# Value rows shifted by one token inside SBUF on ScalarE's queue, and the next dense job's first weights loaded a piece sooner

## The chip, the cores and the metric

The kernel runs on one core of a Trainium2 chip. The core has TensorE (PE, matmuls), VectorE (DVE), ScalarE (ACT), GpSimd (POOL) and SyncE (SP), which here only issues transfers. Sixteen DMA engines move data between DRAM and SBUF, the on-chip memory of 128 partitions. The metric is the device time of one execution in microseconds (us); lower is better.

## The reference

One layer of an encoder over 2048 tokens of width 1024: adaptive RMS norm, one input projection to two groups of eight heads, stick-breaking attention for the first group and chunked softmax attention for the second, an output projection, and a squared-ReLU MLP. The change touches the values of the first group:

```python
h = rmsnorm(x, g_norm1[l]) * (1.0 + sc1) + sh1
proj = h @ w_in[l]
q_sb, k_sb, v_sb, q_ca, k_ca, v_ca = jnp.split(proj, split_pts, axis=-1)
...
    suffix = lax.cumsum(log_1m_beta, axis=3, reverse=True) - log_1m_beta
    w = jnp.where(strict, jnp.exp(log_beta + suffix), 0.0)
    outs.append(jnp.einsum('bhqk,bkhd->bqhd', w.astype(v.dtype), vb))
```

## The kernel before

Tokens are stored in reverse order, in four blocks (`tb` 0 to 3) of `TB` = 512 tokens, each of four tiles of 128 tokens. fp32 products are made of three matmuls on a high and a low part, which the kernel produces with a cast on ACT and a subtraction on DVE (`split`).

A stick-breaking weight is a difference of two neighbouring running products. The kernel doesn't form these differences of weights; it multiplies the running products with differences of values, v(next row) - v(row), and adds the first row of each tile at the end (`vcol`). So for every value tile (`vr`, 128 tokens by 512 columns) it needs the same tile moved up by one row (`vn`). Row 127 of `vn` is the first row of the next tile, and for a block's last tile the first row of the block that was computed before. In the old kernel the whole tile is written to DRAM (`scr_r`) and read back one row further (`raw_rows`, `next_rows`).

The work runs in stages:

- **Projection stage** (about 0 to 443 us). A list of jobs (feature group, piece, block) is run by `run_job`. Piece 4 holds the first group's values; its jobs (0, 4, 3), (0, 4, 2) and, as the last job of all, (1, 4, 1) go through `step_values`. PE fills one of four PSUM banks for each tile; ACT copies it to `vr`; SP issues the write and the read; POOL subtracts; ACT and DVE split the result into `sv`; SP stores it. Two small queues of work, `behind` and `later`, run a piece of work a given number of tiles after it was added. With (0, 10, 2) the norm of block 0 begins: its x goes into the buffers that block 1's x leaves, ACT squares it, DVE sums (`nsaa`), and PE needs the sums (`pva`).
- **Attention stage** (about 443 to 1700 us). Units of scores, sigmoid, scan, transposes and value products, with the rest of the projections and the output projections as filler matmuls between them (`Filler`, `fill_qkv`, `outproj`). The values of block 0 are made here by `late_values`, in two halves of 256 columns, two tiles at a time (`vrf`, `vnf`).
- **MLP stage**, which the change doesn't touch.

PE, ACT, DVE and POOL keep the written order through the class `Ordered`, whose line L42 stands for most instructions in the profile. SP keeps the written order up to the attention stage; after that a scheduler arranges SP's issues. The framework gives the transfers of SP's and ACT's queues, in the order of the program, eight semaphores in turn. A transfer therefore waits on its queue until the transfer eight places before it, on whichever queue, is complete. All loads and stores of the names above are SP's; ACT's queue carried nine transfers.

A filler's weights go through a ring of three buffers (tag `r8`); a piece needs two of them. Inside a job the next piece's two loads are issued during the last tile of a piece (L1020). The first two of a new job are issued when the job starts, after its activations `fx` (L1005 here, in `fill_qkv`):

```python
            ht = self.moving()
            ...
            nxt = [load(pieces[0], i) for i in range(2)]
            yield "wait" if tb == 0 else "start"
```

Of the kernel before, what the change touches and what calls it, by code (L numbers as in the profile page):

```python
# [18 lines left out]
P = 128  # L19
# [60 lines left out]
def encoder_kernel(ctx, tc, xT, c, g1, g2, w_in, w_rest, gqk, bias, w_o, w1, w2, w_ada, b_ada, out):  # L80
# [31 lines left out]
    scr_r = dram.tile([S + P, NH * HD], F32, name="scr_r")  # L112
    scr_h = dram.tile([P, KT, 2, TB], F32, name="scr_h")

    ident = cpool.tile([P, P], F32, name="ident")
# [102 lines left out]
        )  # L218


    def raw_rows(tb, t, n, cols):

        r = tb * TB + t * P
        return scr_r[r : r + n * P, cols].rearrange("(t p) e -> p t e", p=P)

    def next_rows(tb, t, n, cols):

        r = tb * TB + t * P + 1
        return scr_r[r : r + n * P, cols].rearrange("(t p) e -> p t e", p=P)

    def first_values(tb, pairs):

        for pr in pairs:
            src = scr_r[tb * TB : (tb + 1) * TB, pr * P : (pr + 1) * P].rearrange("(i r) p -> p i r", r=P)[:, :, 0:1]
            sp.dma_start(vcol[:, pr, 4 * tb : 4 * tb + 4].unsqueeze(2), src)

    stores, drain = [], []
# [16 lines left out]
    if True:  # L254
# [178 lines left out]
                        later.add(3 + n // 2, lambda n=n: turn(n))  # L433
                yield

        waiting, halves = [], []

        def step_values(tb, tt, ps, nm):

            raw = stp.tile([P, TB], F32, tag="qh", name=f"vr{nm}_{tt}", bufs=6)  # L440
            act.copy(raw, ps)
            sp.dma_start(raw_rows(tb, tt, 1, slice(None))[:, 0], raw)
            waiting.append((tt, raw))
            for n in range(1 if tt < 3 else 2):
                if waiting[0][0] == tt and tt < 3:
                    break
                t, r = waiting.pop(0)
                behind.add(2 + n, lambda t=t, r=r: follow(tb, t, r, nm))
            if tt == 3:
                behind.add(2, lambda: first_values(tb, range(NH // 2)))  # L450

        def follow(tb, t, raw, nm):

            nx = stp.tile([P, TB], F32, tag="qh", name=f"vn{nm}_{t}", bufs=6)
            sp.dma_start(nx, next_rows(tb, t, 1, slice(None))[:, 0])

            def less():
                pool.tensor_tensor(nx, nx, raw, op=ALU.subtract)

            def parts():  # L460
                if t % 2 == 0:
                    halves[:] = [
                        stp.tile([P, NH // 2, 2, 2, HD], F32R, tag="st", name=f"sv{nm}_{t}_{hf}") for hf in range(2)
                    ]
                for hf, sv in enumerate(halves):
                    half = nx[:, hf * CW : (hf + 1) * CW].rearrange("p (h d) -> p h d", d=HD)
                    split(sv[:, :, t % 2, 0, :], sv[:, :, t % 2, 1, :], half)
                    if t % 2:
                        sp.dma_start(
                            scr_v[0, tb, hf][:, :, t - 1 : t + 1, :].rearrange("h p t e -> p h (t e)"),  # L470
                            sv.rearrange("p h t l d -> p h (t l d)").bitcast(F32),
                        )

            behind.add(1, less)
            behind.add(2, parts)

        def prepare_wo(n):
            raw = stp.tile([P, KT, P], F32, tag="bg", name=f"wo{n}", bufs=2)
# [164 lines left out]
        osp.dma_start(scr_r[S, :].rearrange("(p f) -> p f", p=P), vcol[:, 0, : NH * HD // P])  # L643

        todo = [(1.5, lambda j=j: ada(j)) for j in range(2 * KT, 6 * KT)]
        for i in range(NH):
# [66 lines left out]
    if True:  # L713
# [253 lines left out]
        class Filler:  # L967


            def __init__(self, make, *x):  # L970
                self.tiles = []
                self.gen = make(self, *x)
                self.src = next(self.gen)

            def fetch(self, n):

# [16 lines left out]

        def fill_qkv(self, tb, ht, pieces):

            self.tiles = ht or []
            yield None if ht else lambda k: scr_h[:, k]
            ht = self.moving()

            def load(piece, i):  # L1000
                w = ring.tile([P, KT // 2, 2, CW], F32R, tag="r8", name=f"fw{tb}_{piece}_{i}")
                sp.dma_start(w.bitcast(F32), scr_w[piece,][:, i * 4 : i * 4 + 4, :, :])
                return w

            nxt = [load(pieces[0], i) for i in range(2)]  # L1005
            yield "wait" if tb == 0 else "start"
            for n, piece in enumerate(pieces):
                grp, hf = divmod(piece, 2)
                w, nxt = nxt, []
                for j in range(2):  # L1010
                    if n == len(pieces) - 1 and j:
                        yield "ahead"
                    nm = f"f{tb}_{piece}_{j}"
                    ps = dense.tile([P, TB], F32, tag="ps", name=f"p{nm}")
                    last = 0 if grp < 2 else 1
                    for tt in range(last + 1):
                        tl = slice((2 * j + tt) * P, (2 * j + tt + 1) * P)
# [24 lines left out]
                    yield keep  # L1042
# [3 lines left out]
        def late_values(tb, hf, j, ps, nm):  # L1046

            cols = slice(hf * CW, (hf + 1) * CW)
            raw = raws[j] = fp.tile([P, 2, CW], F32, tag="vr", name=f"vr{nm}", bufs=2)
            act.copy(raw, ps.rearrange("p (t c) -> p t c", t=2))  # L1050
            sp.dma_start(raw_rows(tb, 2 * j, 2, cols), raw)
            if not j:
                return
            for i in range(2):
                later.add(1 + i, lambda i=i, raw=raws[i]: late_follow(tb, hf, i, raw, nm))
            later.add(2, lambda: first_values(tb, (2 * hf, 2 * hf + 1)))

        def late_follow(tb, hf, j, raw, nm):

            nx = xrp.tile([P, 2, CW], F32, tag="xr", name=f"vn{nm}_{j}")  # L1060
            sp.dma_start(nx, next_rows(tb, 2 * j, 2, slice(hf * CW, (hf + 1) * CW)))

            def less():
                pool.tensor_tensor(nx, nx, raw, op=ALU.subtract)
# [5 lines left out]
            later.add(1, less)  # L1070
            later.add(2, parts)

        stepped = set()

        def outproj(self, g):
            yield lambda k: scr_m[g, k]

            def load(n):
                w = ring.tile([P, 2, KT, P], F32R, tag="r8", name=f"ow{g}_{n}")
                sp.dma_start(w.bitcast(F32), scr_wo[n,])  # L1080
                return w

            mx = self.moving()
            ws = [load(0), load(1)]
            rx = load_residual(g, 0, xrp)
            yield "wait"
            for n in range(KT):
# [2 lines left out]
                    resident[n] = w  # L1090
                if n + 2 < KT:
                    ws.append(load(n + 2))
                if n + 1 < KT:
                    rx = load_residual(g, n + 1, xrp)
                else:
                    yield "ahead"
# [59 lines left out]
        def fill(part):  # L1156
# [5 lines left out]
            while credit >= 1 and filler and not rest:  # L1162
# [3 lines left out]
                elif got == "ahead":  # L1166
                    for f in filler[1:2]:
                        f.ahead()
                elif callable(got):
# [611 lines left out]
```

## Time and profile before

| | us |
|---|---|
| median of 3 runs (2689.1 to 2690.29) | 2689.9 |
| the profiled execution | 2689.82 |
| its span, first to last instruction | 2688.0 |

| engine | busy us | share |
|---|---|---|
| PE | 2583.0 | 96% |
| DVE | 1884.6 | 70% |
| ACT | 1417.6 | 53% |
| POOL | 604.2 | 22% |

In the page's forty slices of 67.2 us the DMA engines' busy share is highest in the projection stage:

```profile
DMA  9779977988887678775778777796675343465574
```

Each digit is tenths of the 16 DMA engines' time. A row of a group or of the timeline names engine, operation, and the tiles written and read (`out<-in`); behind a bracket or a bar stands the idle time ahead of it and what ended it.

### The profile page before, as it was taken

Reading aid. Unit: us, or ns where it says so; the run is one execution under the profiler, and the core shown is the slowest. Engines: PE = TensorE matmul, PEld = TensorE weight load, DVE = VectorE, ACT = ScalarE, POOL = GpSimd, SP = SyncE. Lnnn points to the kernel's source line nnn. Section 1 sums busy time; section 2 is a strip of 40 time slices with the busy share of each in tenths; the row PEclk is TensorE's granted clock in tenths of the full one; section 3 lists DMA queues with packets and bytes.
Section 4 is the critical chain, followed back from the end, with each engine's and each line's share of the span. In section 5 each row is a group of like instructions: output and inputs, shape, how many; then the busy total and the mean of one; then the engine's idle time right before and its main releaser. Section 6 shows DMA issues by size and latency. Waiting matters only on the chain. (4 is left out here: it accounts for less than half of the span.)

```text
span 2688.0 us, 38753 instructions
## 1 busy us (share of the span) xinstructions
PE 2583.0 (96%) x12816; PEld 2163.1 (80%) x12816; DVE 1884.6 (70%) x3222; ACT 1417.6 (53%) x2722; POOL 604.2 (22%) x617
## 2 busy tenths in 40 slices
PE   6999797899899899999999999999999999999999
PEld 5888686779788788878888888878888888888887
DVE  6655574678689787989758878767857565655565
ACT  5333333776676577656665444456544444444443
POOL 4331142421430134111442232200001323200000
PEclk9999898999999899999999999999999999999999
DMA  9779977988887678775778777796675343465574
GB/s 344 299 299 346 343 282 250 285 259 256 265 258 252 210 228 288 226 246 184 218 258 295 271 265 260 254 335 216 219 270 188 138 164 138 149 243 191 201 266 157
DMA packets 277272, 659.59 MB, mean 245 GB/s; under 512 B 38736, under 2 KB 72528, under 8 KB 267216
## 3 DMA queue, kind: packets, MB, share of 16 engines
q1 hardware_dynamic: 275776, 652.40, 71.3%
q10 hardware_dynamic: 1296, 4.72, 0.4%
q8 instruction: 101, 1.65, 0.3%
q14 instruction: 99, 0.81, 0.1%
HBM read 461.44 MB, written 195.56 MB: 244 GB/s over the span
## 5 line engine op out<-in xcount | busy, mean ns | idle before, releaser
L42 PE MATMUL ps<-oph,opv 128*128 128x512 f32 x2688 | 612.3, 389 | 0.2
L42 PE MATMUL ps<-h,opw 128*128 128x512 f32 x2664 | 606.3, 390 | 2.6 <-DVE cx L42 2.6
L42 PEld LDWEIGHTS ps<-oph,opv 128*128 128x128 f32 x2688 | 503.8, 188 | 106.8 <-DVE opv L42 1.2
L42 PEld LDWEIGHTS ps<-h,opw 128*128 128x128 f32 x2664 | 501.0, 188 | 107.6 <-DVE cx L42 3.5
L42 ACT CAST wth<-wt 128x512 fp32r<-128x512 f32 (+3 forms) x544 | 257.1, 483 | 215.3 <-PE wt L42 205.7
L42 DVE TENSOR_TENSOR wtl<-wt,wth 128x512 fp32r<-128x512 f32 (+3 forms) x544 | 291.3, 547 | 82.0 <-ACT wth L42 79.9
L42 DVE TENSOR_TENSOR oph<-hw,oph 128x512 fp32r<-128x512 f32 x224 | 156.2, 697 | 221.0 <-ACT oph L42 221.0
L42 PE MATMUL pt<-w,ht 128*128 128x512 f32 x1248 | 291.5, 393 | 2.8 <-DVE qh L42 2.2
L42 ACT CAST oph<-hw 128x512 fp32r<-128x512 f32 x224 | 139.3, 622 | 282.8 <-PE ps L42 264.8
L42 PEld LDWEIGHTS pt<-w,ht 128*128 128x128 f32 x1248 | 234.5, 189 | 52.5 <-ACT csq L42 2.9
L42 DVE TENSOR_TENSOR_SCAN p<-z,p,zero 128x512 f32<-128x512 f32 x192 | 245.4, 1278 | 34.9 <-ACT z L42 33.9
L42 PE MATMUL acc<-wth,v 128*128 128x512 f32 (+3 forms) x544 | 222.0, 412 | 2.3 <-DMA v<-scr_v 2.3
L42 PE MATMUL z<-k,q 128*128 128x512 f32 (+3 forms) x640 | 186.8, 374 | 29.9 <-DVE p L42 27.5
L42 ACT ACTIVATE z<-z 128x512 f32<-128x512 f32 (+1 forms) x320 | 166.2, 520 | 60.2 <-PE z L42 54.9
L42 POOL TENSOR_TENSOR ts<-w 128x512 f32<-128x512 f32 x32 | 46.0, 1437 | 662.3 <-DMA w<-in_w_dram 557.0
L42 PE MATMUL acc<-wtl,v 128*128 128x512 f32 (+3 forms) x544 | 186.3, 349 | 0.0
L42 DVE TENSOR_TENSOR opw<-w,opw 128x512 fp32r<-128x512 f32 x127 | 101.8, 803 | 113.0 <-ACT opw L42 112.8
L42 POOL TENSOR_TENSOR e<-e,cols 128x640 f32<-128x640 f32 (+4 forms) x128 | 143.0, 1123 | 163.4 <-DVE cols L42 84.0
L42 PE MATMUL wt<-ident,p 128*128 128x128 f32 x1088 | 172.2, 274 | 4.4 <-DVE cols L42 2.9
L42 PEld LDWEIGHTS wt<-ident,p 128*128 128x128 f32 x1088 | 134.8, 141 | 35.3 <-DVE cols L42 5.7
L42 PE MATMUL po<-fx,ow 128*128 128x512 f32 x576 | 160.3, 393 | 0.0
L42 PEld LDWEIGHTS z<-k,q 128*128 128x128 f32 x640 | 115.1, 191 | 52.5 <-DVE p L42 31.5
(197 smaller groups left out, 3963.9 us busy)
## 6 DMA issues: line engine op xcount, KB each, us to landing
hw<-scr_hid SPq DMA_DIRECT2D x112, 512.0 KB, 4.1
k<-scr_k SPq DMA_DIRECT2D x272, 128.0 KB, 4.3
v<-scr_v SPq DMA_DIRECT2D x136, 256.0 KB, 3.8
q<-scr_q SPq DMA_DIRECT2D x128, 256.0 KB, 5.1
w<-in_w_dram SPq DMA_DIRECT2D x64, 512.0 KB, 5.4
hw<-scr_s SPq DMA_DIRECT2D x64, 512.0 KB, 4.6
fw<-scr_w SPq DMA_DIRECT2D x28, 1024.0 KB, 6.9
wa<-in_w_ada_dram SPq DMA_DIRECT2D x48, 512.0 KB, 6.2
```

Of the source, the lines that this page charges most:

```text
L42: return lambda *x, **y: self.tc.keep_in_program_order(f(*x, **y))
```

## The change

1. In `step_values` and `late_values` the tile `vn` is made without DRAM. ACT's queue issues one transfer of 127 rows from `vr` to `vn`, one row higher (`step_down`), and one for the last row, from the next tile's first row (`step_over`). The first row of each tile goes to a small DRAM tensor `scr_f` (`first_row`), from which a block's last tile gets its last row (`next_block`) and `vcol` its columns. `scr_r`, `raw_rows` and `next_rows` are gone.
2. The subtraction and the split stand at other places of `behind` and `later`, and `vcol` is read later.
3. A filler holds its first two weight loads in `firsts`. The filler that runs yields `"weight"` twice while its last piece runs, and the next one issues one load each time.

```diff
-    def raw_rows(tb, t, n, cols):
...
-    def next_rows(tb, t, n, cols):
...
+    def step_down(nx, raw):
+
+        act.dma_start(nx[0 : P - 1], raw[1:P])
+
+    def step_over(nx, raw):
+
+        act.dma_start(nx[P - 1 : P], raw[0:1])
...
         def step_values(tb, tt, ps, nm):
 
             raw = stp.tile([P, TB], F32, tag="qh", name=f"vr{nm}_{tt}", bufs=6)
+            if tb > 1:
+                nx = stp.tile([P, TB], F32, tag="qh", name=f"vn{nm}_{tt}", bufs=6)
+            elif tt % 2:
+                nx = before["pair"][:, 1]
+            else:
+                before["pair"] = stp.tile([P, 2, TB], F32, tag="bg", name=f"vn{nm}_{tt}", bufs=2)
+                nx = before["pair"][:, 0]
             act.copy(raw, ps)
-            sp.dma_start(raw_rows(tb, tt, 1, slice(None))[:, 0], raw)
-            waiting.append((tt, raw))
...
+            step_down(nx, raw)
+            act.dma_start(first_row(tb, tt, slice(None)), raw[0:1])
+            if tt:
+                step_over(before[tt - 1][1], raw)
+            before[tt] = raw, nx
+            if tt:
+                behind.add(1, lambda: follow(tt - 1, nm))
             if tt == 3:
-                behind.add(2, lambda: first_values(tb, range(NH // 2)))
-
-        def follow(tb, t, raw, nm):
-
-            nx = stp.tile([P, TB], F32, tag="qh", name=f"vn{nm}_{t}", bufs=6)
-            sp.dma_start(nx, next_rows(tb, t, 1, slice(None))[:, 0])
-
-            def less():
-                pool.tensor_tensor(nx, nx, raw, op=ALU.subtract)
+                act.dma_start(nx[P - 1 : P], next_block(tb, slice(None)))
+                behind.add(1, lambda: follow(tt, nm))
+                behind.add(4, lambda: first_values(tb, range(NH // 2)))
...
+            def weight(self):
+                if self.firsts:
+                    self.got.append(self.firsts.pop(0)())
...
-                            if n + 1 < len(pieces) and j and tt == last and k in (0, 4):
-                                nxt.append(load(pieces[n + 1], k // 4))
+                            if j and tt == last and k in (0, 4):
+                                if n + 1 < len(pieces):
+                                    nxt.append(load(pieces[n + 1], k // 4))
+                                else:
+                                    yield "weight"
...
         def late_values(tb, hf, j, ps, nm):
...
+            nx = xrp.tile([P, 2, CW], F32, tag="xr", name=f"vn{nm}")
             act.copy(raw, ps.rearrange("p (t c) -> p t c", t=2))
-            sp.dma_start(raw_rows(tb, 2 * j, 2, cols), raw)
+            step_down(nx, raw)
+            step_over(nx[:, 0], raw[:, 1])
+            for t in range(2):
+                act.dma_start(first_row(tb, 2 * j + t, cols), raw[0:1, t])
+            if j:
+                step_over(raws[0][1][:, 1], raw[:, 0])
+                act.dma_start(nx[P - 1 : P, 1], next_block(tb, cols))
```

PE's instructions stand in the same order in both kernels. Three places show how the other queues change. In a row, `vr_4_3_0` is the raw tile of piece 4, block 3, tile 0 (the last number is the buffer's), `pt` its PSUM bank, and the sizes are those of the tile written.

ACT, at the first value job of the projection stage, before:

```order
L42 COPY vr_4_3_0_2152<-pt_4_3_0_2127 128x512
L42 COPY vr_4_3_1_2190<-pt_4_3_1_2165 128x512
L42 COPY vr_4_3_2_2230<-pt_4_3_2_2205 128x512
L42 COPY vr_4_3_3_2263<-pt_4_3_3_2238 128x512
L42 COPY vr_4_2_0_2297<-pt_4_2_0_2272 128x512
L42 CAST sv_4_3_0_0_2301<-vn_4_3_0_2236 128x4x64
```

The same place of ACT now:

```order
L42 DMA vn_4_3_0_2153<-vr_4_3_0_2152 127x512
L42 DMA scr_f<-vr_4_3_0_2152 1x512
L42 COPY vr_4_3_1_2192<-pt_4_3_1_2167 128x512
L42 DMA vn_4_3_1_2193<-vr_4_3_1_2192 127x512
L42 DMA scr_f<-vr_4_3_1_2192 1x512
L42 DMA vn_4_3_0_2153<-vr_4_3_1_2192 1x16x32
L42 COPY vr_4_3_2_2236<-pt_4_3_2_2211 128x512
L42 DMA vn_4_3_2_2237<-vr_4_3_2_2236 127x512
L42 DMA scr_f<-vr_4_3_2_2236 1x512
L42 DMA vn_4_3_1_2193<-vr_4_3_2_2236 1x16x32
L42 CAST sv_4_3_0_0_2245<-vn_4_3_0_2153 128x4x64
```

Two or three transfers now stand behind each copy in ACT's own order, and the first cast of a shifted tile stands after three copies and not after five. The third transfer of tile 1 (16 pieces of 32 columns, the last row of tile 0's `vn`) takes the same semaphore as the first one, eight places before it.

ACT, at the end of the last value job, where the first scores `z` of the attention stage follow; before:

```order
L42 COPY vr_4_1_3_3986<-pt_4_1_3_3961 128x512
L42 CAST sv_4_1_0_0_3995<-vn_4_1_0_3941 128x4x64
L42 CAST sv_4_1_0_1_3996<-vn_4_1_0_3941 128x4x64
L42 CAST sv_4_1_0_0_3995<-vn_4_1_1_3989 128x4x64
L42 CAST sv_4_1_0_1_3996<-vn_4_1_1_3989 128x4x64
L42 CAST sv_4_1_2_0_4017<-vn_4_1_2_4001 128x4x64
L42 CAST sv_4_1_2_1_4018<-vn_4_1_2_4001 128x4x64
L42 CAST sv_4_1_2_0_4017<-vn_4_1_3_4003 128x4x64
L42 CAST sv_4_1_2_1_4018<-vn_4_1_3_4003 128x4x64
L42 ACTIVATE z_0_3_3_0_3992<-z_0_3_3_0_3992 128x512
```

The same place now:

```order
L42 COPY vr_4_1_3_4007<-pt_4_1_3_3982 128x512
L42 DMA vn_4_1_2_3952<-vr_4_1_3_4007 127x512
L42 DMA scr_f<-vr_4_1_3_4007 1x512
L42 DMA vn_4_1_2_3952<-vr_4_1_3_4007 1x16x32
L42 DMA vn_4_1_2_3952<-scr_f 1x512
L42 CAST sv_4_1_0_0_3957<-vn_4_1_0_3871 128x4x64
L42 CAST sv_4_1_0_1_3958<-vn_4_1_0_3871 128x4x64
L42 CAST sv_4_1_2_0_4028<-vn_4_1_2_3952 128x4x64
L42 CAST sv_4_1_2_1_4029<-vn_4_1_2_3952 128x4x64
L42 CAST sv_4_1_2_0_4028<-vn_4_1_2_3952 128x4x64
L42 CAST sv_4_1_2_1_4029<-vn_4_1_2_3952 128x4x64
L42 ACTIVATE z_0_3_3_0_4021<-z_0_3_3_0_4021 128x512
```

Four transfers come in between; the casts of the shifted tiles stand ahead of the first score in both, six now and eight before, since tile 0's two casts moved up by one tile.

SP, around the first weights of block 0's filler job in the attention stage (`fw_2_0`, `fw_2_1`); before:

```order
L215 DMA scr_v_1_1_151<-svf_11_1_7052 128x4x256
L982 DMA fx_4_7061<-scr_h 128x1024
L982 DMA fx_5_7063<-scr_h 128x1024
L982 DMA fx_6_7065<-scr_h 128x1024
L982 DMA fx_7_7067<-scr_h 128x1024
L1002 DMA fw_2_0_7069<-scr_w_222 128x2048
L1002 DMA fw_2_1_7071<-scr_w_222 128x2048
L733 DMA q_3_2_7103<-scr_q_2_1_101 64x1024 x2
```

The same place of SP now:

```order
L790 DMA scr_m_2_174<-os_5_2_3_6916 128x1024
L1016 DMA fw_2_0_6925<-scr_w_222 128x2048
L759 DMA v_7_2_3_6933<-scr_v_3_1_147 128x512
L1016 DMA fw_2_1_6984<-scr_w_222 128x2048
L742 DMA q_2_2_6992<-scr_q_2_1_101 64x1024 x2
L750 DMA k_2_2_6995<-scr_k_2_1_133 64x512 x2
L750 DMA k_2_2_6995<-scr_k_3_1_137 64x512 x2
```

The two loads stand one unit of the attention sooner, ahead of q and k of a unit and of the four `fx` loads.

More of the change, by code (lines that the diff above doesn't have):

```diff
@@ L111, in encoder_kernel @@
     scr_b = scratch("scr_b", [P, WIN], NH)
-    scr_r = dram.tile([S + P, NH * HD], F32, name="scr_r")
+    scr_f = dram.tile([4 * NTB + 1, NH * HD, 1], F32, name="scr_f")
     scr_h = dram.tile([P, KT, 2, TB], F32, name="scr_h")
@@ L469, in parts @@
                         sp.dma_start(
-                            scr_v[0, tb, hf][:, :, t - 1 : t + 1, :].rearrange("h p t e -> p h (t e)"),
+                            scr_v[0, int(nm[-1]), hf][:, :, t - 1 : t + 1, :].rearrange("h p t e -> p h (t e)"),
                             sv.rearrange("p h t l d -> p h (t l d)").bitcast(F32),
                         )
-            behind.add(1, less)
-            behind.add(2, parts)
+            behind.add(1, parts)
         def prepare_wo(n):
@@ L642, in encoder_kernel @@
         osp.dma_start(gqk_sb, gqk)
-        osp.dma_start(scr_r[S, :].rearrange("(p f) -> p f", p=P), vcol[:, 0, : NH * HD // P])
+        osp.dma_start(scr_f[4 * NTB].rearrange("(p f) o -> p (f o)", p=P), vcol[:, 0, : NH * HD // P])
         todo = [(1.5, lambda j=j: ada(j)) for j in range(2 * KT, 6 * KT)]
@@ L970, in __init__, with weights @@
             def __init__(self, make, *x):
-                self.tiles = []
+                self.tiles, self.firsts, self.got = [], [], []
                 self.gen = make(self, *x)
                 self.src = next(self.gen)
+            def weight(self):
+                if self.firsts:
+                    self.got.append(self.firsts.pop(0)())
+            def weights(self):
+                while self.firsts:
+                    self.weight()
+                return self.got
             def fetch(self, n):
@@ L994, in fill_qkv @@
         def fill_qkv(self, tb, ht, pieces):
-            self.tiles = ht or []
-            yield None if ht else lambda k: scr_h[:, k]
-            ht = self.moving()
             def load(piece, i):
@@ L1003, in load @@
                 return w
-            nxt = [load(pieces[0], i) for i in range(2)]
+            self.tiles = ht or []
+            self.firsts = [lambda i=i: load(pieces[0], i) for i in range(2)]
+            yield None if ht else lambda k: scr_h[:, k]
+            ht = self.moving()
+            nxt = self.weights()
             yield "wait" if tb == 0 else "start"
@@ L1048, in late_values @@
             cols = slice(hf * CW, (hf + 1) * CW)
[L1049 removed]
+            raw = fp.tile([P, 2, CW], F32, tag="vr", name=f"vr{nm}", bufs=2)
+            nx = xrp.tile([P, 2, CW], F32, tag="xr", name=f"vn{nm}")
             act.copy(raw, ps.rearrange("p (t c) -> p t c", t=2))
[L1051 removed]
+            step_down(nx, raw)
[5 more added lines that the diff above has]
+                act.dma_start(nx[P - 1 : P, 1], next_block(tb, cols))
+            raws[j] = raw, nx
             if not j:
@@ L1054, in late_values, with late_follow @@
             for i in range(2):
[L1055 to L1064, printed above, removed]
+                later.add(2 + i, lambda i=i, r=raws[i]: late_follow(tb, hf, i, *r, nm))
+            later.add(6, lambda: first_values(tb, (2 * hf, 2 * hf + 1)))
+        def late_follow(tb, hf, j, raw, nx, nm):
+            pool.tensor_tensor(nx, nx, raw, op=ALU.subtract)
             def parts():
@@ L1068, in parts @@
                 stepped.add((tb, hf, j))
-            later.add(1, less)
-            later.add(2, parts)
+            later.add(1, parts)
         stepped = set()
         def outproj(self, g):
-            yield lambda k: scr_m[g, k]
             def load(n):
@@ L1081, in load @@
                 return w
+            self.firsts = [lambda n=n: load(n) for n in range(2)]
+            yield lambda k: scr_m[g, k]
             mx = self.moving()
-            ws = [load(0), load(1)]
+            ws = self.weights()
             rx = load_residual(g, 0, xrp)
@@ L1092, in outproj @@
                     ws.append(load(n + 2))
+                elif g > 1:
+                    yield "weight"
                 if n + 1 < KT:
@@ L1168, in fill @@
                         f.ahead()
+                elif got == "weight":
+                    for f in filler[1:2]:
+                        f.weight()
                 elif callable(got):
```

20 lines of the change are left out of this document (9 added, 11 removed).

## The prediction

> **What bounds the kernel now.** Read first the busy times, then who TensorE (PE) waits for.
>
> ```profile
> PE 2583.0 (96%) x12816; PEld 2163.1 (80%) x12816; DVE 1884.6 (70%) x3222; ACT 1417.6 (53%) x2722; POOL 604.2 (22%) x617
> PE pva L42 <- DVE nsaa L42: 27.9, 2, 15.4
> PE z L42 <- DVE p L42: 27.5, 9, 14.1
> PE pf L42 <- DMA fw<-scr_w: 8.1, 1, 8.1
> ```
>
> PE is the bound: 105 of the 2688.0 us are idle, and its instructions stand in the same order after the change. So the time moves only by what PE waits, and the change touches the longest waits. The next views are timelines of these places, and the windows there.
>
> ```profile
> 221.45 0.57 ACT L42 COPY vr<-pt 128x512 f32<-128x512 f32 x1
> 301.28 1.29 POOL L42 TENSOR_TENSOR vn<-vn,vr 128x512 f32<-128x512 f32 x1 [13.39 <-DMA vn<-scr_r]
> 319.65 1.87 PE L42 MATMUL pva<-ones,nsaa 128*128 128x1 f32 x8 [15.41 <-DVE nsaa L42]
> 222.00:320.00 98.00, 81.97 (x367) 67.13 (x365) 47.09 (x81) 29.37 (x64) 13.20 (x17) 0.94 1.00 351
> 320.00:330.00 10.00, 10.00 (x36) 8.35 (x36) 7.36 (x14) 5.68 (x12) 1.42 (x4) 0.69 0.77 273
> ```
>
> Call this **place 1**. From the first value copy (ends 222.0) to the norm of block 0 (319.65) eight value tiles go to DRAM and come back; the last comes at 301.28, 18.4 us before PE goes on. Behind it stand ScalarE's (ACT's) casts, the free buffers for x of block 0, its load and its squares. In the window row the columns are PE, PEld, DVE, ACT, POOL, clock, DMA share, GB/s: the 16 DMA engines are full (1.00) for all 98 us. Any DMA work that the change adds here has nothing to hide behind, and any it takes away is time. After the wait the clock is 0.69 for 10 us: 36 matmuls, where 367 in 81.97 us make 45 at full clock, 2 us lost.
>
> ```profile
> 424.10 0.59 ACT L42 COPY vr<-pt 128x512 f32<-128x512 f32 x1 [4.42 <-PE pt L42]
> 452.28 2.63 POOL L42 TENSOR_TENSOR vn<-vn,vr 128x512 f32<-128x512 f32 x2 [0.94 <-DMA vn<-scr_r]
> 455.56 1.39 ACT L42 ACTIVATE z<-z 128x512 f32<-128x512 f32 x4
> 457.44 1.22 PE L42 MATMUL z<-k,q 128*128 128x512 f32 x2 [14.07 <-DVE p L42]
> 420.00:450.00 30.00, 23.37 (x114) 19.52 (x113) 7.58 (x15) 5.30 (x10) 4.57 (x8) 0.93 0.76 240
> ```
>
> **Place 2**: the last four value tiles stand ahead of the first sigmoid in ACT's order, so PE's 14.07 us end with their last landing. **Place 3** is the same in the attention loop, twice, and **place 4** the weights that come late:
>
> ```profile
> 881.37 0.59 ACT L42 COPY vrf<-pf 128x512 f32<-128x512 f32 x1
> 885.00:895.00 10.00, 3.90 (x21) 3.08 (x20) 2.96 (x6) 2.84 (x6) 2.58 (x3) 0.89 0.71 209
> 891.71 0.62 ACT L42 CAST svf<-vnf 128x512 fp32r<-128x512 f32 x1 [7.16 <-POOL vnf L42]
> 893.83 1.22 PE L42 MATMUL z<-k,q 128*128 128x512 f32 x2 [6.11 <-DVE p L42]
> 922.67 0.60 ACT L42 COPY vrf<-pf 128x512 f32<-128x512 f32 x1
> 931.76 0.62 ACT L42 CAST svf<-vnf 128x512 fp32r<-128x512 f32 x1 [4.11 <-POOL vnf L42]
> 681.86 2.74 SPq L982 DMA_DIRECT2D fx<-scr_h  x4
> 684.64 1.34 SPq L1002 DMA_DIRECT2D fw<-scr_w  x2
> 694.73 3.36 PE L42 MATMUL pf<-fx,fw 128*128 128x512 f32 x7 [8.06 <-DMA fw<-scr_w]
> ```
>
> **What a moved tile costs.** The change replaces a write and a read of 256 KB by one transfer of 127 rows from SBUF to SBUF, and two of a single row (the first row to DRAM, the last row from the next tile or from DRAM). Before has no transfer of 127 rows and none within SBUF. How are transfers dealt out?
>
> ```profile
> q1 hardware_dynamic: 275776, 652.40, 71.3%
> q10 hardware_dynamic: 1296, 4.72, 0.4%
> scr_w<-w ACTq DMA_DIRECT2D x8, 512.0 KB, 9.9
> scr_m<-os ACTq DMA_DIRECT2D x1, 512.0 KB, 6.2
> scr_r<-vr SPq DMA_DIRECT2D x12, 256.0 KB, 5.0
> vn<-scr_r SPq DMA_DIRECT2D x12, 256.0 KB, 5.1
> vnf<-scr_r SPq DMA_DIRECT2D x4, 256.0 KB, 3.5
> ```
>
> Queue q10 is ACT's: 8 + 1 transfers made 1296 packets, 144 each. A tile has 128 rows, so 16 packets are left, one for each engine: 128 rows go in 16 equal shares of 8. 127 is a prime number. In equal shares it goes to one engine or to 127, and there are 16. So either the shares are unequal (nearly a sixteenth each) or one engine carries all 127 rows of 2 KB, 0.260 MB. The prices: in place 1 the 16 engines move 351 GB/s, one of them 21.9, so 0.260 MB take **11.9 us** on one engine and 0.74 us on sixteen. By q1's row (652.40 MB in 71.3% of 16 x 2688 us, 47.0 us per MB and engine) it is 12.2. Rows within SBUF go to no DRAM, which may make them a little cheaper; I take 11, with 10 and 12.2 as ends. I choose one engine, since the only row on shares shows equal ones. The Trainium skill has a rule on this in "DMA: Bandwidth & Descriptors", section "Why a DMA increments its semaphore by 16 and not by 1": a transfer from SP's or ACT's queue uses the largest number of engines up to 16 that divides the outer dimension on both sides, and 127 partitions are named there as a case with one engine, always the lowest-numbered. By that rule the sum is the one below, by the 16 shares of q10's rows it would be the second rival's; no run here shows it.
>
> **Place 1.** Eight transfers of 127 rows: 8 x 11 = 88 us more on one engine. It is no longer asked to carry its part of the 16 removed transfers of 256 KB: 4.2 MB at 351 GB/s, 12 us. A tile that is dealt over 16 engines is complete when the slowest has its part, so that one engine sets the pace for SP's queue too, and before it was already full (1.00). The x of block 0 comes behind all of this in SP's order, so place 1 grows by 88 - 12 = **76 us**. Two couplings keep it from being hidden. ACT's order is fixed: the casts of w_10, which PE's next eight tiles need, stand behind a transfer that waits for the sixth value tile; PE has four PSUM banks of lead, then it stands. And each transfer waits until the one eight places before it, on either queue, is complete; the trace shows SP held by that:
>
> ```profile
> SPq L42 <- DMA scr_w<-w: 7.6, 10, 2.9
> 222.42 10.52 SPq L42 DMA_DIRECT2D scr_w<-w  x8
> 855.00 0.33 SPq L750 DMA_DIRECT2D v<-scr_v  x1
> ```
>
> Now ACT's instructions are held by it as well: the short last-row transfer of tile 0 waits for tile 0's 127 rows (same semaphore), with the copy of tile 2 behind it. The bounds: if SP's transfers gave way entirely, the eight end at 222 + 88 = 310, plus 18.4 gives 328, **9 us** later than 319.65; with 12.2 each and nothing saved, 98 us. The full share of 1.00 is nearest to the upper part; I take 76. The 15.4 us of waiting are inside these figures, not an extra gain.
>
> **Place 2.** Four transfers, 44 us on one engine from 424.7. SP loads q, k and weights meanwhile: share 0.76 of the 27.6 us to 452.3 is 21 us, less 6 for eight removed transfers, 15. The last tile lands between 424.7 + 44 = 469 and 424.7 + 59 = 484 instead of about 452: +16 to +32, and I take **+30**, since SP's transfers here are asked ahead of the last two value tiles. ACT's cast and the first sigmoids stay behind it.
>
> **Place 3.** From copy to cast 10.3 and 9.1 us now. Afterwards copy 0.6, 11 on one engine, 4 for half of what SP has on that engine meanwhile (0.71 of 11), and POOL's subtraction 1.3: 17. That is 6.7 + 7.9 = **+15**; ACT's wait passes to PE (7.16 became 6.11). Ends: 0 to +25. ACT now issues 56 transfers more itself, 24 of them in place 1 and ten for each pair of late tiles; no row has an issue of ACT's, SP's shortest is 0.33 us, so a late pair costs ACT some 3 us (inside these ends) and place 1 some 8, where ACT is busy 29 of 98 us.
>
> **Place 4.** The two weight loads leave during the previous piece, ahead of the hidden-state loads. The 8.06 us go; next late are the four fx tiles (asked at 681.86 to 684.6), of which the first is needed only at the fifth weight block. With a faster restart I count **-7**; ends 0 and -10. The load waits in SP's in-order queue until PE frees a ring buffer, and q, k of the next units are behind it; they are two units ahead.
>
> All else (subtractions, casts, vcol's reads) is the same count at another position.
>
> **The sum.** From the profiled execution, 2689.82 us (span 2688.0 plus 1.8; the median of the runs is 2689.9): + 76 + 30 + 15 - 7 = +114, **2804 us**.
>
> **The rivals.**
> 1. *Dealt nearly evenly*: 127 rows take a few us, as the 128-row ones. Place 1's wait goes (15.4 and 2 for the clock), place 2 ends after about four issues, a landing of 5 and POOL's 1.3, 6 us earlier; place 3 gains 8, place 4 gains 7: 38. ACT, now held by SP's slow loads, gives back some 5: **2657 us**, faster. It decides from the point at which a 127-row transfer lands within the time of one tile, 24 matmuls (5.4 us by 367 in 81.97). For it: the 16 shares of q10. Against it: they are equal.
> 2. *One engine, but SP's transfers give way*: 9 + 16 + 7 - 7 = +25, **2715 us**. For it: much of SP's load is for later jobs. Against: SP's order is kept.
> 3. *One engine, and idle between steps*: each of the 16 value transfers also pays a landing of 5 us, because the next is issued only when an earlier one is complete: +80, **2884 us**.
> 4. *The early weights alone matter*, because the value path is hidden: 2683 us. Against it: the waits above have the value tiles as their releaser.
>
> **Chances.** Forecast 0.70, rival 1 0.13, rival 2 0.10, rival 3 0.05, rival 4 0.02. The range takes in the forecast and rival 2 with their unknown prices: 2710 to 2880. Faster 0.14, same 0.01, slower 0.85; bounds of 0.2% are 5.4 us, about what a measurement of this kernel can tell from no change.
>
> **What would show it.** q10's packets: a 127-row transfer on one engine closes with one packet, not 16; its landing in the table of issues would be 11 us or more, against 5.0. POOL's last vn of place 1 would begin after 340, the waits of PE there would sum to 60 us or more, and the DMA share there would fall though PE waits. The wait on fw<-scr_w must be gone. If the landing is near 5 us, the choice on the shares was wrong and rival 1 holds; if it is long and the time below 2730, the cover was.

## The result and the profile after

The changed kernel takes **2822.4 us** (median of 4 runs, 2821.0 to 2828.2) against 2690.1 for the kernel before on the same chip: 1.0493 times as long, 95% interval 1.0475 to 1.0512. The prediction was 2804, in a range of 2710 to 2880. The profiled execution took 2821.5, its span is 2819.5; 131.5 us more than before have to be found.

First the page of the changed kernel: the engines, the DMA share in 40 slices, the packets and megabytes of SP's queue (q1) and ACT's (q10). Then who PE waits for (total, times, longest).

```profile
PE 2594.6 (92%) x12816; PEld 2171.4 (77%) x12816; DVE 1882.1 (67%) x3222; ACT 1418.5 (50%) x2722; POOL 600.3 (21%) x617
DMA  9874488488897737977577777777667334465564
q1 hardware_dynamic: 270144, 644.01, 67.0%
q10 hardware_dynamic: 3874, 8.95, 0.8%
```

```profile
PE z L42 <- DVE p L42: 68.3, 13, 26.9
PE pva L42 <- DVE nsaa L42: 37.8, 2, 25.6
PE pra L42 <- DVE ndga L42: 31.3, 2, 28.0
PE pt L42 <- ACT w L42: 29.9, 1, 29.9
```

PE executes the same 12816 matmuls in 11.6 us more (the clock granted over the span is 0.963, before 0.987); the rest of the loss is waiting. The line on `fw<-scr_w` is gone from this view. Of the DMA share the fourth, fifth and eighth slice, each 9 before, show 4. SP's queue moves 8.4 MB less: the 32 removed transfers of 256 KB.

Now place by place, on the timeline and in the window of place 1 (columns as in the prediction). PE's order is the same in both kernels, so the start of the same matmul, after minus before, is the loss up to there.

```profile
287.41 2.04 PE L42 MATMUL pra<-ndga,ones 128*128 128x128 f32 x8 [27.98 <-DVE ndga L42]
319.31 46.77 PE L42 MATMUL pt<-w,ht 128*128 128x512 f32 x192 [29.86 <-ACT w L42]
391.71 1.87 PE L42 MATMUL pva<-ones,nsaa 128*128 128x1 f32 x8 [25.63 <-DVE nsaa L42]
561.96 1.22 PE L42 MATMUL z<-k,q 128*128 128x512 f32 x2 [26.91 <-DVE p L42]
790.04 1.78 PE L42 MATMUL pf<-fx,fw 128*128 128x512 f32 x7
969.65 1.22 PE L42 MATMUL z<-k,q 128*128 128x512 f32 x2 [8.51 <-DVE p L42]
995.21 0.69 PE L42 MATMUL z<-k,q 128*128 128x128 f32 x2 [6.61 <-DVE p L42]
1027.82 1.22 PE L42 MATMUL z<-k,q 128*128 128x512 f32 x2 [5.58 <-DVE p L42]
1059.94 1.22 PE L42 MATMUL z<-k,q 128*128 128x512 f32 x2 [13.16 <-DVE p L42]
```

```profile
343.72 2.54 POOL L42 TENSOR_TENSOR vn<-vn,vr 128x512 f32<-128x512 f32 x2 [11.55 <-DMA vn<-vr]
222.00:320.00 98.00, 38.83 (x171) 31.41 (x169) 12.21 (x24) 8.97 (x20) 8.33 (x12) 0.71 0.39 134
```

| place | from rows | us | predicted |
|---|---|---|---|
| 1 | 391.71 - 319.65 | +72.1 | +76 |
| 2 | 561.96 - 457.44 - 72.1 | +32.4 | +30 |
| 4 | 790.04 - 694.73 - 104.5 | -9.2 | -7 |
| 3, and all behind it | 131.5 - 95.3 | +36.2 | +15 |

In place 1 three waits of PE have taken the place of one. The last two subtractions begin at 343.72, not at 301.28. And in the window the DMA engines are used at 0.39 where they were full, while PE stands: something is slow that uses few of them.

The packets say what. Queue q10 has 2578 packets more than before. If a transfer of 127 rows closes once, 16 of them make 16 x (127 + 1); the 15 last rows from a neighbouring tile, each cut into 16 pieces, 15 x (16 + 16); the 25 single rows from or to DRAM 25 x 2: 2048 + 480 + 50 = 2578. With 16 closings each it would be 2818. So each transfer of 127 rows ran on **one engine**. The trace's packet records agree: the rows of the first three tiles lie between 226.47 and 262.93 us, mostly 0.080 us apart (2 KB, 25.6 GB/s), and their durations sum to 32.3 us in 36.5. That is 12.2 us a tile, one behind the other. (The records name the queue and not the engine; that it is one follows from the closing packets.) Over all eight tiles of place 1 the packets of 2 KB sum to 88.4 us, but they reach from 226.47 to 342.91: 116.4 us, 14.6 a tile. Between tiles stand only gaps of 2.3, 2.0 and 0.6 us; most of the rest lies between one row and the next.

Who stands behind that engine is in two more views of place 1: ACT's issues on the timeline (start, duration), and what SP's queue waited for between 200 and 345 us.

```profile
224.86 6.40 ACTq L42 DMA_DIRECT2D vn<-vr  x1
231.30 10.05 ACTq L42 DMA_DIRECT2D scr_f<-vr  x1
243.29 8.38 ACTq L42 DMA_DIRECT2D scr_f<-vr  x1
```

```profile
SPq L42 <- DMA vn<-vr: 73.6, 5, 26.0
SPq L42 <- DMA scr_f<-vr: 22.7, 2, 11.7
```

SP's transfers there neither read nor write `vn` or `vr`; they take the semaphore of an ACT transfer eight places before and wait for it. The semaphore numbers in the trace show it: `scr_w<-w`, issued at 249.69, waits for the semaphore that `vn<-vr`, issued at 224.86, had taken. SP stands 96 us, and ACT up to 10 us at an issue, with its copies and casts behind. So the x of block 0, which stands behind this in SP's order, is issued 73 us later (first before, then after), although the last value tile is only 42 us later (343.72, before 301.28):

```profile
305.31 5.31 SPq L42 DMA_DIRECT2D xt<-in_xT_dram  x8
378.36 5.28 SPq L42 DMA_DIRECT2D xt<-in_xT_dram  x8
```

### The profile page after: what moved, and what is told of

Read it like the earlier page. It is cut to its first block, busy times and chain, and to the rows that moved or that the text cites. A ratio compares the mean times of both kernels' runs of the same rounds, so it can differ in the third digit from the quotient of the medians.

```text
span 2819.5 us, 38757 instructions
## 1 busy us (share of the span) xinstructions
PE 2594.6 (92%) x12816; PEld 2171.4 (77%) x12816; DVE 1882.1 (67%) x3222; ACT 1418.5 (50%) x2722; POOL 600.3 (21%) x617
## 5 line engine op out<-in xcount | busy, mean ns | idle before, releaser
L42 PE MATMUL pt<-w,ht 128*128 128x512 f32 x1248 | 294.9, 396 | 33.3 <-ACT w L42 29.9
```

The costliest lines, as they stand in the source:

```text
L42: return lambda *x, **y: self.tc.keep_in_program_order(f(*x, **y))
```

## The experiments

Each kernel is timed against the kernel before on the same chip; the ratio's 95% interval stands behind the median. The edits are against the changed kernel unless said otherwise. The runs were taken on four chips, on which the median of the kernel before was 2689.5 to 2694.5, so a difference of a few us between runs of two chips says nothing.

| run | us | ratio to before |
|---|---|---|
| the changed kernel | 2822.4 | 1.0475 to 1.0512 |
| e1_split | 2678.3 | 0.9946 to 0.9973 |
| e2_sp | 2788.1 | 1.0344 to 1.0384 |
| e3_weights | 2676.9 | 0.9930 to 0.9967 |
| e4_late | 2718.7 | 1.0083 to 1.0126 |
| e5_two | 2738.8 | 1.0166 to 1.0202 |
| e6_late_sp | 2706.7 | 1.0048 to 1.0087 |
| e7_place2 | 2714.0 | 1.0077 to 1.0117 |
| e8_half | 2722.2 | 1.0107 to 1.0138 |
| e9_split_x | 2678.2 | 0.9934 to 0.9965 |
| e10_dram_x | 2677.0 | 0.9926 to 0.9964 |
| e11_mixed_x | 2674.0 | 0.9926 to 0.9953 |
| e12_pool | 2661.8 | 0.9862 to 0.9909 |

### One engine, or ACT's queue? (e1_split, e2_sp)

```diff
-        act.dma_start(nx[0 : P - 1], raw[1:P])
+        act.dma_start(nx[0:112], raw[1:113])
+        act.dma_start(nx[112 : P - 1], raw[113:P])
```

> The changed kernel, with each transfer of 127 rows made as two, of 112 rows (16 times 7) and of 15 rows. Theory A (one engine carries a 127-row transfer, and that is what places 1 to 3 pay): the wide transfers take 1 to 2 us plus their landing, the last value of place 1 is subtracted before 300 us, the longest PE waits of place 1 shrink to below those of the kernel before (15.4), and the time is 2650 to 2690. On ACT's queue 16 more transfers close with 16 x 30 = 480 more packets: 4354 in all. Theory B (what costs is ACT's queue, held by 56 transfers with eight shared semaphores, however many engines carry them): 16 transfers more on that queue can't help, the time stays at 2800 or above.

```diff
-        act.dma_start(nx[0 : P - 1], raw[1:P])
+        sp.dma_start(nx[0 : P - 1], raw[1:P])
```

> The changed kernel, with the 16 transfers of 127 rows issued by SP's queue; the short ones stay on ACT's. Theory A (one engine): the same rows go through the same single engine, place 1 stays 55 to 85 us late, and the time is 2790 to 2830. Theory B (ACT's held queue): ACT's copies and casts are free of the wide transfers, and the time falls to below 2740.

With more transfers on the same queue, but dealt out, the loss is gone: 144 us less than the changed kernel. With the wide transfers on SP's queue most of it stays. 2788 is just below the expected 2790: 34 us less than the changed kernel, about half of them in place 3. Place 1 is 65.9 us late by the norm's matmul (385.50, before 319.65). Theory A stands.

```profile
385.50 1.87 PE L42 MATMUL pva<-ones,nsaa 128*128 128x1 f32 x8 [21.19 <-DVE nsaa L42]
```

In e1_split's page ACT's queue has exactly the expected packets:

```profile
q10 hardware_dynamic: 4354, 8.95, 1.0%
```

A's expectation holds, but its point on PE's wait holds barely. On e1_split's timeline the value path of place 1 is done 33 us before its time in the kernel before, and PE's wait is nearly what it was (13.22, before 15.41):

```profile
268.08 2.73 POOL L42 TENSOR_TENSOR vn<-vn,vr 128x512 f32<-128x512 f32 x2 [3.03 <-DMA vn<-vr]
303.27 5.75 SPq L42 DMA_DIRECT2D xt<-in_xT_dram  x8
309.36 0.63 ACT L42 ACTIVATE nsaa<-xt 128x512 f32<-128x512 f32 x1 [11.57 <-DMA xt<-in_xT_dram]
316.54 1.87 PE L42 MATMUL pva<-ones,nsaa 128*128 128x1 f32 x8 [13.22 <-DVE nsaa L42]
```

ACT is idle for 11.57 us until x of block 0 lands, which SP issues at 303.27. In the kernel before it did so at 305.31, only 2 us later. So the value tiles were not all that PE waited for there: without them, too, other transfers in SP's order keep x until about this time.

### How many rows on the busiest engine (e5_two, e8_half)

```diff
-        act.dma_start(nx[0 : P - 1], raw[1:P])
+        act.dma_start(nx[0:122], raw[1:123])
+        act.dma_start(nx[122 : P - 1], raw[123:P])
```

> The changed kernel, with each transfer of 127 rows made as two, of 122 rows (2 times 61) and of 5 rows: as many transfers as in e1_split. If the outer dimension is dealt over the largest number of engines that divides it, the wide part closes with 2 packets and the small one with 5 (16 x 6 = 96 more packets on ACT's queue than in the changed kernel: 3970), and the busiest engine carries 61 rows a tile and not 8. Theory C (the busiest engine's rows set the pace where the DMA engines are full: 0.080 us a row, 8 tiles, as +72 in place 1 is near 8 x 119 x 0.080 = 77 less what e1_split had to spare): place 1 is 8 x 53 x 0.080 = 34 less 4 = 30 us later than in e1_split, places 2 and 3 some 8 each, and the time is 2725 (2705 to 2745). Theory D (a tile costs nothing as long as its transfer ends within the time of one tile of matmuls, 5.4 us; 61 rows take 4.9): 2678 to 2690.

e8_half is e1_split with a third argument for `step_down`: where it is true, the 127 rows go in one transfer, otherwise in 112 and 15.

```diff
+            step_down(nx, raw, tb == 3)
```

> e1_split, with the transfer of 127 rows kept whole for the four tiles of the first value job (half of place 1) alone. Theory C (full engines, so every row on the busiest one is time): 4 x 119 x 0.080 = 38 less 4, the time is 2712 (2700 to 2722). If there is room for four such transfers and only the eight in a row overrun it, 2678 to 2690.

ACT's queue in e5_two has the 3970 packets of the expectation, so 122 rows and 5 rows together closed seven times (two and five). The norm's matmul in e5_two and in e8_half:

```profile
q10 hardware_dynamic: 3970, 8.95, 0.9%
359.89 1.86 PE L42 MATMUL pva<-ones,nsaa 128*128 128x1 f32 x8 [15.46 <-DVE nsaa L42]
```

```profile
356.91 1.87 PE L42 MATMUL pva<-ones,nsaa 128*128 128x1 f32 x8 [10.74 <-DVE nsaa L42]
```

Against e1_split's 316.54, with the rows that the busiest engine carries above eight a tile, at 0.080 us:

| kernel | rows above | x 0.080 us | measured |
|---|---|---|---|
| e8_half | 4 x 119 | 38 | 40.4 |
| e5_two | 8 x 53 | 34 | 43.4 |
| the changed kernel | 8 x 119 | 76 | 75.2 |

Place 1 grows with the rows on the busiest engine, and there is no room for even four such transfers. Theory D's time is missed (2739 against 2690 at most), but so is its condition: by the packet records a tile's rows in e5_two took 6.4 to 11.4 us, not 4.9, so whether a landing within one tile's 5.4 us would make a transfer free stays open. Both expected times were too low, e8_half's by 10 us and just out of its bounds (2722.2 against 2722). The 4 us that both took off, as what e1_split seemed to have to spare, are a part of that. Two engines cost 9 us more than the rows; why was not tried.

### Place 2 and place 3 by themselves (e7_place2, e4_late, e6_late_sp)

e7_place2 uses the same argument for the last value job:

```diff
+            step_down(nx, raw, tb == 1)
```

> e1_split, with the transfer of 127 rows kept whole for the four tiles of the last value job (place 2) alone. If place 2's term is what it seems in the changed kernel's trace (+32.4, predicted +30), the time is 2678 + 33 = 2711 (2703 to 2718). If most of it came from place 1 (its late copies and loads), 2680 to 2695.

35.7 us above e1_split, and the wait of place 2 in its timeline is the changed kernel's (26.91) almost to the digit:

```profile
487.24 1.22 PE L42 MATMUL z<-k,q 128*128 128x512 f32 x2 [27.21 <-DVE p L42]
```

The next two start from the kernel before. e4_late takes over `step_down`, `step_over`, `late_values` and `late_follow` from the changed kernel, with the first rows in `scr_r`; e6_late_sp has `sp.dma_start` for each `act.dma_start` in them.

> The kernel before, with block 0's late values alone made the new way (four transfers of 127 rows and 20 short ones on ACT's queue; first rows go to the old DRAM tensor). If place 3 costs what the changed kernel's trace shows between its first score wait at 970 us and its last at 1060 us, the time is 2690 + 36 = 2726 (2718 to 2734). By the prediction's term (only the second pair of each half is paid) it is 2705 (2698 to 2712). If those waits come from the delay of the earlier places, it is 2690.

> e4_late, with all 24 transfers of the late values issued by SP's queue. Theory E (what the prediction missed in place 3 is ACT, held at its own issues of short transfers while a 127-row one has the engine: 3.9 + 3.8 + 5.0 + 5.5 us in e4_late): ACT is never held, and the time is 2690 to 2706. Theory F (the landing on one engine alone makes the wait, whichever queue issues it): as e4_late, 2712 to 2725. SP's queue carries the loads of q and k as well; if it is held in ACT's place and these come late, PE waits for them and the time is 2725 or above.

The late values have 20 transfers in all, four of 127 rows and 16 short ones, not the 24 of the two expectations. e4_late is 29.2 us above the kernel before (22 to 34 by the interval), at the lower bound of the first expectation (2718). e6_late_sp is 16.3 above (13 to 23). By the view of the tile `vrf`, "who waited for it" (total, times), in e4_late and in e6_late_sp:

```profile
  POOL vnf L42: 58.0, 2
  ACT z L42: 35.4, 4
  ACT svf L42: 7.2, 1
```

```profile
  POOL vnf L42: 63.5, 2
  ACT svf L42: 28.8, 2
```

In e4_late ACT's sigmoids (`z`) stand four times behind transfers that ACT itself issues, once for each pair of tiles; in e6_late_sp only the casts `svf` wait, twice, for the landing. On PE's timeline of e6_late_sp these are the two waits

```profile
899.43 1.22 PE L42 MATMUL z<-k,q 128*128 128x512 f32 x2 [14.18 <-DVE p L42]
952.82 0.79 PE L42 MATMUL z<-k,q 128*128 128x512 f32 x1 [11.55 <-DVE p L42]
```

together 25.7, where the kernel before has 6.11 and about 3.7: 16 us more, the whole of e6_late_sp's loss. Neither theory alone is right: the landing on one engine is worth 16 us, and issuing from ACT, which then stands at its own issues, about 12 more.

### The early weights alone (e3_weights)

The kernel before with part 3 of the change (`firsts`, `weight`, `weights`, `"weight"`) and nothing else.

> The kernel before, with the next dense job's first two weight loads a piece early and nothing else changed. If the loads are hidden there as they are in the changed kernel, the wait of PE for fw (8.06 us) goes and the time is 2680 to 2685. If what follows (the hidden states fx, or q and k of the next units behind the loads in SP's order) is late in turn, it stays within 3 us of 2690.

12.6 us faster than before (9 to 19 by the interval): more than the 8.06 us of the wait. The wait is gone in its timeline too; 8.8 us are found there, the rest in pieces of 1 to 3 us at other places, too small to give a cause.

### Is there anything to gain in place 1? (e9_split_x, e10_dram_x, e11_mixed_x)

This edit is added to e1_split in e9_split_x and to e3_weights in e10_dram_x; e11_mixed_x is e9_split_x with the late values by way of DRAM.

```diff
-                        2 + m // 4,
+                        (6 if p == 10 else 2) + m // 4,
```

> e1_split, with the 16 stores of w_10 to DRAM (scr_w, 4.2 MB) issued four tiles later, behind the load of block 0's x in SP's order. In e1_split the last value tile of place 1 is done at 268 us and the x buffers are free at 290, but SP issues that load at 303.3, behind these stores, and PE's wait for nsaa (12 to 13 us) is as long as before. Theory G (place 1's wait was never the value path's alone: the load of x stands behind full DMA engines in SP's order): the load leaves at 290 to 294, the wait falls below 5 us, the time is 2669 (2665 to 2673). If the stores only come back as another wait (full engines, w buffers), it stays 2675 to 2681.

> e3_weights (values by way of DRAM), with the same 16 stores four tiles later. They stood ahead of the last two reads of value tiles as well. If these stores are all that made the value path late in the kernel before, this gains what e9 gains: 2668 (2664 to 2672), and the way through SBUF is worth nothing in place 1 even dealt over 16 engines. If the round trip through DRAM is late by itself, the x buffers come free near 303 to 308 as before, and the time stays 2674 to 2680.

> e9_split_x, with the late values (place 3) by way of DRAM as in the kernel before. In e1_split place 3 lost about 3 us to ACT's own issues and e3_weights lost none there, so 3 us below e9_split_x: 2666 (2662 to 2670). If ACT's issues there cost nothing, as e9_split_x.

In e9_split_x x is issued at 291.85 and the wait that was in question is gone. The next rows on PE's timeline:

```profile
305.53 1.05 PE L42 MATMUL pva<-ones,nsaa 128*128 128x1 f32 x8 [0.21 <-DVE nsaa L42]
317.55 10.64 PE L42 MATMUL pt<-w,ht 128*128 128x512 f32 x33 [6.36 <-ACT w L42]
```

The norm comes 11.0 us sooner than in e1_split; 6.36 of it are lost at once on the next weights' casts, and by the medians nothing is left: 2678.2 against 2678.3. Theory G is right about the wait and wrong about the time. The six executions reach from 2670.8 to 2682.5, and the traced one is the quickest of them, so the trace can't show where the rest goes.

For the values by way of DRAM it is 2677.0 against e3_weights' 2676.9. That is the time of the second case of e10_dram_x's expectation, but not its cause. With the stores out of the way x is issued at 294.52 there, not near 305, and the wait nearly goes:

```profile
308.21 1.05 PE L42 MATMUL pva<-ones,nsaa 128*128 128x1 f32 x8 [2.43 <-DVE nsaa L42]
```

So the round trip through DRAM is not late by itself, and here too the shorter wait brings no measurable time. e11_mixed_x is 4 us below e9_split_x, inside the spread of both (2670 to 2682): undecided.

### Another queue (e12_pool)

```diff
-        act.dma_start(nx[0 : P - 1], raw[1:P])
+        pool.dma_start(nx[0 : P - 1], raw[1:P])
```

> The changed kernel, with the 16 transfers of 127 rows issued by POOL's queue, which has semaphores of its own; the short ones stay on ACT's. In the changed kernel SP stood 96 us in place 1 behind transfers of ACT's queue (73.6 + 22.7), because the semaphores are shared in turn, while the DMA share fell to 0.39. Theory K (the shared semaphores hand the one engine's backlog on to SP and ACT): with the same rows on one engine, but nobody else waiting for their semaphores, SP's waits for these transfers go, the DMA share of 222 to 320 us returns above 0.8, and the time is 2700 to 2765. Theory L (the engine's backlog alone, through the share of every other transfer that it carries): as e2_sp or the changed kernel, 2785 to 2825. If POOL's queue deals the rows over many engines (its packets close more than once a transfer), it is as e1_split, 2670 to 2690, and says nothing on the semaphores.

The fastest of all: **2661.8 us** (2659.1 to 2663.7), 0.9886 times the kernel before. It was the third case of the expectation, though better than its 2670: POOL's queue (q0 on the page) deals the rows.

```profile
q0 software_dynamic: 1280, 4.16, 0.5%
313.05 1.87 PE L42 MATMUL pva<-ones,nsaa 128*128 128x1 f32 x8 [11.70 <-DVE nsaa L42]
445.85 1.22 PE L42 MATMUL z<-k,q 128*128 128x512 f32 x2 [8.67 <-DVE p L42]
871.55 0.73 PE L42 MATMUL z<-k,q 128*128 128x512 f32 x2 [0.73 <-DVE p L42]
```

16 transfers make 1280 packets, 80 each: by the packet records 64 with data, nearly all of 4 KB, and 16 closings. Those of one tile sum to 13.45 us and lie within 1.28 us (421.79 to 423.07), so at least ten engines worked at once. This overlap shows the dealing. The expectation's sign, more than one closing packet, does not by itself: no run shows how a transfer closes on POOL's queue that is not dealt. Place 2 ends with a wait of 8.67 instead of 14.07, and in place 3 the 6.11 us before are 0.73. Against e1_split it has the wide transfers in one piece, 32 transfers fewer on ACT's queue, and semaphores apart from SP's and ACT's (numbers 111 to 118 in the trace, where those use 100 to 107); which of these is worth how much of the 16.5 us was not separated. Since the rows are no longer on one engine, the run doesn't tell whether the shared semaphores alone would have carried the delay to SP and ACT (theories K and L stay open).

## Why the prediction was right, and where it was off

- **The one engine** (the choice on which all rested): shown. 127 rows close with one packet, 112 and 15 together with 31, 122 and 5 together with seven. This is the rule that the prediction took from the Trainium skill, "DMA: Bandwidth & Descriptors", section "Why a DMA increments its semaphore by 16 and not by 1", and the trace agrees with it in all three cases: 1, 16 + 15, 2 + 5. The price of 11 us a tile is what its packets sum to (88.4 us for eight); beside the other packets the first three tiles took 12.2 us each and all eight 14.6. Two slips change nothing: by 16 shares the sum would be that of the first rival in the list (2657), not of the second, and the 45 matmuls in 10 us that are called full clock come from a row with a clock of 0.94.
- **Place 1**, +76: +72.1. The size holds, and so does its proportion to the rows (e8_half, the table above). What was argued loosely is why nothing hides it. The prediction led with the DMA engines being full; in fact they are full no longer (0.39), since SP's queue stands 96 us behind ACT's transfers. That coupling was named, as one that keeps the cost from being hidden, and it is what the profile after shows. That the sum comes within 4 us is in part luck: it took 88 us for the eight tiles (they took 116.4) and 12 off for the removed transfers (no run shows that saving), and what came out is a last value tile 42 us late and x issued 73 us late.
- **Place 2**, +30: +32.4 in the trace, 35.7 by itself (e7_place2). Right.
- **Place 3**, +15: +36.2 with all that follows it. **This is the term that was mis-sized**, beyond its own end of +25, and nearly the whole error: 2821.5 - 2804 is 17.5 us, this term's is 21. By itself (e4_late) place 3 is 29.2; where the 7 us more in the changed kernel come from was not tried. The prediction followed the path from copy to cast of the second pair of each half, and e6_late_sp shows that part at 16 us. It put ACT's own issues at "some 3 us" for a late pair, inside the ends (and counted ten for each pair; there are four or six, ten for each half). But ACT isn't busy with an issue, it stands there: 8.6 us at the first pair's first-row transfers in the changed kernel, with the sigmoids behind it, and the first pair of each half, which the prediction left out, delays PE as well. The step forgot what it had said of place 1, that an issue waits for the transfer eight places before, where it mattered most: in front of the engine that feeds PE.
- **Place 4**, -7: -9.2 in the trace, -12.6 for the edit alone (e3_weights). Right in kind, a little small.
- **The rivals.** Even dealing (2657) did not happen in the changed kernel, but e1_split and e12_pool make it happen. e1_split's 2678 shows one step of that rival to be wrong: it counted place 1's 15.4 us as the value path's own, and they were x's load in SP's order too. e12_pool's 2662 comes near 2657, by way of places 2 and 3 and the weights. That SP gives way (2715) and that only the weights matter (2683) are refuted by the trace after; for idle landings between steps (2884) there is no sign: in place 1 the gaps between the eight tiles sum to 4.9 us, where this rival asks 5 for each tile.

The list of signs held as far as it can be read: one closing packet, the last subtraction after 340 (343.72), waits of PE in place 1 above 60 us (29.9 + 28.0 + 25.6), a lower DMA share while PE waits, and no wait for `fw`. The landing of 11 us or more can't be read from the table of issues, which gives no landing times for the changed kernel; the rows' 12.2 to 14.6 us a tile stand in for it.

These 8.6 us, on ACT's timeline of the changed kernel:

```profile
957.72 1.24 ACTq L42 DMA_DIRECT2D vnf<-vrf  x2
959.00 8.60 ACTq L42 DMA_DIRECT2D scr_f<-vrf  x2
```

## What to carry to other kernels

Before a transfer is moved to another queue, work out over how many engines its shape is dealt on that queue: with the same 127 rows the kernel took 2822 us on ACT's queue, 2788 on SP's, 2678 in two pieces of 112 and 15, and 2662 on POOL's. On ACT's queue the packets that close a transfer told it without any timing (1, 31 and 7 here); on POOL's it took the packets' times. And where transfers share semaphores in turn, a slow one stops the queue that comes round to its semaphore; on a computing engine that stops the instructions behind the issue as well.

When a wait ends with a certain transfer, look for what else ends just before it: in place 1 taking 33 us off the value tiles let SP issue x's load only 2 us sooner, and brought next to nothing.

## What was not expected of the hardware

- POOL's queue deals 127 rows over many engines at once, in packets of 4 KB, where ACT's has packets of 2 KB on one engine. The Trainium skill has this too, in the section named above: an exception by which some plain copies issued by POOL are dealt over 16 engines with the rows rounded up, 127 among its examples. The trace agrees as far as it shows (ten at once, 1.28 us).
- A transfer that isn't held costs ACT 0.64 us of its own time with 127 rows (at 496.26 in the changed kernel) and 0.26 with one row (at 222.79); a held one up to 10.05.
- The whole way of the values through SBUF, dealt out on ACT's queue, is worth nothing measurable against the way through DRAM: e1_split 2678.3, e3_weights 2676.9, though it moves 4.2 MB less (655.4 against 659.6 on the two pages).
